# Transposing the second feed-forward's activation by VectorE in 32x32 blocks

## The chip, the cores and the metric

The kernel runs on one core of a Trainium2 chip, in one launch. The metric is the device time of one execution in microseconds (us): the median of three runs. PE is TensorE (matrix products, with PEld for its weight loads), DVE is VectorE, ACT is ScalarE, SP is the engine that issues the DMAs. Each engine works through its own instructions in the order in which the program emits them and waits for the others by semaphores.

## The reference, cut to what matters

The program is two transformer blocks of width 2048 over 256 tokens, float32. Each ends in a feed-forward of width 8192; the change touches the second one, whose result is the kernel's output:

```
h2 = rms_norm_2(x, norm2_w[l]) * (1.0 + scale2) + shift2
ff = jnp.square(jax.nn.relu(h2 @ w_ff1[l])) @ w_ff2[l]
x  = x + gate2 * ff
```

`scale2`, `shift2` and `gate2` come from a matrix product of a condition vector with `w_ada`, which the kernel does on VectorE.

## The kernel before, in words

**The stream.** All weights come from HBM as one stream of 1 MB blocks of 128 x 4 x 512 floats. A block has two halves, and a half-block holds two units; a unit is one 128x512 weight tile that is multiplied with the activations of both token tiles (`tt` 0 and 1, 128 tokens each). Float32 is split in two rounded parts: `prep_hi` (L183) lets ACT write the high part of a half-block (L201), `prep_lo` (L205) lets DVE write the remainder (L209). Each unit is then three products for each token tile (L303 to L305: high by high, high by low, low by high), so a half-block is 12 products. `hi` and `lo` have four buffers each (`HLB`), and `run` (L245) emits the split of a half-block three half-blocks before its products (`LOOK`).

**The second feed-forward** (`ffn`, L403) goes in four chunks `c` of 2048 hidden features. A chunk is first four segments of FF1 (512 hidden features each), then four segments of FF2 (512 output features each). A segment is 16 units, 8 half-blocks, in one accumulator per token tile. In chunk 0 the first two FF1 segments are interleaved block by block (`add_pair`), so that they end one half-block apart.

**The hand-over from FF1 to FF2.** When an FF1 segment's last product is emitted, `ff1_end` emits relu and square on ACT for both token tiles (L419, L420; tile `relu` in SBUF) and starts a generator `go`. FF2 needs this activation transposed, with the hidden features on the partitions. `split_to` (L343) does it for one token tile: four TensorE transposes into a PSUM tile `ms` (L348), ACT's copy to the high part (L349), DVE's subtraction for the low part (L350). The result is the tile `f`. FF2's segment for output group g reads `f` of the four FF1 segments in order, units 0 to 3 from the first, units 12 to 15 from the last.

**What sets the order.** Side work is written as generators. `step` (L238) advances each by one `yield`; `run` calls it twice in each half-block:

```
self.step()
...
self.prep_to(s + 1 + LOOK)
...
self.unit(*todo[0][0])
self.step()
self.unit(*todo[0][1])
```

`go` waits two yields (`lag(2)`), so its work stands in the program at the start of the second half-block after the segment's end. On ACT and DVE that lies between the splits of weights which belong to half-blocks three and four later.

**Other work on DVE here.** `ada_product` (L177) is a 128x2048 product and sum for the next modulation values, emitted ahead of the split of certain blocks: sixteen of these fall in chunks 0 and 1 (`ada2[80:]`, from block 302 on, one in two or three blocks; the second feed-forward is blocks 296 to 423). PSUM is used up: four buffers of `acc` and four of `ms`.

Of the kernel before, what the change touches and what calls it, by code (L numbers as in the profile page):

```python
# [8 lines left out]
F32 = mybir.dt.float32  # L9
# [5 lines left out]
ALU = mybir.AluOpType  # L15
# [3 lines left out]
P = 128  # L19
# [39 lines left out]
def lag(n):  # L59
    for _ in range(n):  # L60
        yield


class Net:
# [278 lines left out]
    def split_to(self, src, dst):  # L343
# [5 lines left out]
        nc.scalar.copy(dst[:, :, 0, :], ps)  # L349
        nc.vector.tensor_tensor(out=dst[:, :, 1, :], in0=ps, in1=dst[:, :, 0, :].bitcast(F32), op=ALU.subtract)  # L350

    def gate_rows(self, col, dst):

        nc = self.nc
        yield from lag(3)
        ps = self.ms([16, P])
        nc.tensor.transpose(ps, col, self.ident)
        row = self.t2([16, P], name="grow")
        nc.scalar.copy(row, ps)
        gd = self.dramp.tile([16, P], F32, tag="gd", name="gd")  # L360
        nc.sync.dma_start(out=gd, in_=row)
        yield from lag(3)
        nc.sync.dma_start(out=dst, in_=gd.rearrange("a b -> (a b)").partition_broadcast(P))
# [36 lines left out]
                norm.stats(0)  # L400


    def ffn(self, w1p, w1, w2, norm, mod, b, ada_base, next_norm=None, out=None):  # L403
        nc = self.nc
        first = len(self.subs)
        norm.attach(first)
        st = {}

        def pools():
            self.phase(fp=4, ffp=1)  # L410
        self.at(first, pools)

        def ff1_end(ft, g):
            def end(acc):
                f = ft[g] = self.fp.tile([P, 4, 2, S], F32R, tag="f", name="f")
                rs = []
                for tt in range(2):
                    r = self.t2(name="relu")
                    nc.scalar.activation(r, acc[tt], AF.Relu)  # L419
                    nc.scalar.activation(r, r, AF.Square)  # L420
                    rs.append(r)

                def go():
                    yield from lag(2)
                    for tt in range(2):
                        self.split_to(rs[tt], f[:, :, :, tt * P:(tt + 1) * P])
                self.spawn(go())
            return end

        def make_gate():  # L430
            assert self.ada_done >= ada_base + 96
            st["gate"] = self.ffp.tile([P, D], F32, tag="gate", name="gate2")
            col = self.mod_cols(mod, b, 80, "gate2c")
            yield
            yield from self.gate_rows(col, st["gate"])

        def early(g, c):
            def end(acc):
                if "sum" not in st:
                    st["sum"] = self.ffp.tile([P, 2, D], F32, tag="sum", name="fsum")  # L440
                cs = slice(g * 512, (g + 1) * 512)
                for tt in range(2):
                    d = st["sum"][:, tt, cs]
                    if c == 0:
                        nc.scalar.copy(d, acc[tt])
                    else:
                        nc.vector.tensor_tensor(out=d, in0=acc[tt], in1=d, op=ALU.add)
                if c == 2:
                    def go():
                        for tt in range(2):  # L450
                            yield from lag(2)
                            d, x = st["sum"][:, tt, cs], self.x[:, tt, cs]
                            nc.vector.tensor_tensor(out=d, in0=d, in1=st["gate"][:, cs], op=ALU.mult)
                            nc.vector.tensor_tensor(out=x, in0=x, in1=d, op=ALU.add)
                    self.spawn(go())
            return end

        def late(g):
            def end_tt(a, tt):
                self.residual(g, a, tt, st["gate"], next_norm)  # L460
                if out is not None:
                    cs = slice(g * 512, (g + 1) * 512)
                    nc.sync.dma_start(out=out[tt, :, cs], in_=self.x[:, tt, cs])
            return end_tt

        for c in range(4):
            ft = {}
            segs = [Seg(norm.lhs, range(16), ff1_end(ft, g)) for g in range(4)]
            if c == 0:
                self.add_pair([w1p[i] for i in range(8)], *segs[:2])  # L470
            else:
                for g in range(2):
                    self.add_seg([w1[4 * c + g, i] for i in range(4)], segs[g])
            for g in (2, 3):
                self.add_seg([w1[4 * c + g, i] for i in range(4)], segs[g])
            if c == 2:
                self.at(len(self.subs) - 24, lambda: self.spawn(make_gate()))
            f_lhs = self.lhs_of(lambda i, ft=ft: ft[i])
            for g in range(4):
                seg = Seg(f_lhs, range(16), early(g, c)) if c < 3 else Seg(f_lhs, range(16), end_tt=late(g), tail=4 if next_norm and g == 3 else 2)  # L480
                self.add_seg([w2[c, g, i] for i in range(4)], seg)
# [849 lines left out]
class Norm:  # L1331


    def __init__(self, net, w_name, mod, b, j_shift, j_scale, ada=0):
        self.n, self.w_name, self.mod, self.b, self.j, self.ada = net, w_name, mod, b, (j_shift, j_scale), ada
        self.ss = net.fix.tile([P, 2, 4], F32, tag="ss", name="ss", bufs=2)
        self.r = net.fix.tile([P, 2], F32, tag="nr", name="nr", bufs=2)
        self.get, self.lhs = net.act_tiles()
        self.xn = {}
        self.after = None  # L1340
# [77 lines left out]
def net(tc, A, out):  # L1418
    with ExitStack() as ctx:
        n = Net(ctx, tc, A)  # L1420
        with tc.manual_schedule():
            n.phase(mixp=1)
            n.setup()
            norm = n.block1()
            norm2 = Norm(n, "norm1_w_2", n.mod2, "b_ada_2", 0, 16, 96)
            n.ffn(A["ff1p_1"], A["ff1_1"], A["ff2_1"], norm, n.mod1, "b_ada", 0, next_norm=norm2)
            norm3 = Norm(n, "norm2_w_2", n.mod2, "b_ada_2", 48, 64, 96)
            n.block2(norm2, norm3)
            n.ffn(A["ff1p_2"], A["ff1_2"], A["ff2_2"], norm3, n.mod2, "b_ada_2", 96, out=out)
            ada2 = [(A["ada2"][j], j, n.mod2, lambda: n.cb) for j in range(96)]  # L1430
            r = n.ada_rest
            n.interleave([(37, 2, r[:4]), (45, 1.05, r[4:34]), (77, 3, r[34:36]), (83, 1, r[36:48]),
                          (100, 1.6, r[48:]), (127, 1, [n.load_c2]), (129, 1, [n.silu_c2]),
                          (130, 1.6, ada2[:58]), (230, 2.6, ada2[58:80]), (302, 2.5, ada2[80:])])
            n.run()
            n.scope.close()
# [118 lines left out]
```

## Time and profile before

| | |
|---|---|
| median of 3 runs | 2510.61 us (2510.32 to 2511.57) |
| profiled execution | 2512.52 us, span 2510.7 us |
| PE busy | 2478.9 us, 99% of the span |
| PE weight loads | 2047.1 us, 82% |
| DVE busy | 1807.3 us, 72% |
| ACT busy | 1259.9 us, 50% |

The span is what the hardware profiler saw of one execution. A busy time is the sum over an engine's instructions; products on PE overlap, so that one lasts 0.39 us while the next starts 0.23 us after it. Starts in a timeline are counted from the span's start. The FF1 segments of the second feed-forward end between about 1835 us (chunk 0) and 2418 us (the last of chunk 3).

### The profile page before, as it was taken

The numbers are of one execution on the slowest core, as the hardware profiler recorded it, in microseconds if no ns is written. First come the engines' busy times: TensorE is split into PE (matmuls) and PEld (weight loads), VectorE is DVE, ScalarE is ACT, GpSimd is POOL, SyncE is SP. The second block draws the span as 40 slices with busy tenths as digits, with TensorE's granted clock in tenths as the row PEclk, the third lists the DMA queues.
The fourth block names the chain that finished last, engine by engine and source line by source line (L and its number), as shares of the span: only waits on it lengthen the run. The fifth ranks groups of instructions, "written<-read, shape, count | busy, mean of one in ns | idle before, by whom it ended". The sixth has DMA issues, their size and how long they took to land.

```text
span 2510.7 us, 29213 instructions
## 1 busy us (share of the span) xinstructions
PE 2478.9 (99%) x11332; PEld 2047.1 (82%) x11332; DVE 1807.3 (72%) x2122; ACT 1259.9 (50%) x1727; POOL 4.0 (0%) x8
## 2 busy tenths in 40 slices
PE   7999999999999999999999999999999999999999
PEld 5778888887888888888887888888788888888887
DVE  7898888888875777787778878766676655456554
ACT  4536645445545444534446556665554453453443
POOL 0000000000000000000000000000000000000000
PEclk9999999999999999999999999999999999999999
DMA  9988678977887778787776655666567655555553
GB/s 358 369 322 318 243 297 323 394 306 286 303 317 284 303 315 316 287 333 306 294 276 222 249 214 211 221 232 223 212 252 278 259 200 194 208 185 191 193 190 130
DMA packets 93580, 666.24 MB, mean 265 GB/s; under 512 B 10817, under 2 KB 11521, under 8 KB 12929
## 3 DMA queue, kind: packets, MB, share of 16 engines
q1 hardware_dynamic: 93442, 664.38, 69.7%
q8 instruction: 89, 1.46, 0.2%
q14 instruction: 49, 0.40, 0.0%
HBM read 660.11 MB, written 4.23 MB: 265 GB/s over the span
## 4 chain that ended last, share of the span: by engine, by line
PE 88%; DVE 6%; ACT 3%; DMA 1%; issue 1%; SPq 0%; ACTq 0%; DVEq 0%
PE acc L303 28%; PE acc L305 28%; PE acc L304 28%; DVE lo L209 2%; DVE ada L177 2%; PE ms L348 1%; DMA raw<-in_win 1%; ACT hi L201 1%; PE ms L1178 1%; PE ms L855 1%; PE ms L1292 0%; ACT hm L1396 0%; PE ms L1410 0%; DVE res L395 0%; PE ms L762 0%
## 5 line engine op out<-in xcount | busy, mean ns | idle before, releaser
L209 DVE TENSOR_TENSOR lo<-raw,hi 128x1024 fp32r<-128x1024 f32 x848 | 1027.6, 1223 | 594.7 <-ACT hi L201 591.6
L201 ACT CAST hi<-raw 128x1024 fp32r<-128x1024 f32 x848 | 884.7, 1051 | 868.1 <-PE acc L305 825.0
L303 PE MATMUL acc<-hi,act 128*128 128x512 f32 x2208 | 875.5, 396 | 7.6 <-ACT hi L201 6.1
L304 PE MATMUL acc<-lo,act 128*128 128x512 f32 x2208 | 864.3, 391 | 9.8 <-DVE lo L209 9.8
L305 PE MATMUL acc<-hi,act 128*128 128x512 f32 x2208 | 863.1, 391 | 0.0
L304 PEld LDWEIGHTS acc<-lo,act 128*128 128x128 f32 x2208 | 416.3, 189 | 99.7 <-DVE lo L209 17.2
L303 PEld LDWEIGHTS acc<-hi,act 128*128 128x128 f32 x2208 | 416.2, 188 | 94.9 <-ACT hi L201 8.4
L305 PEld LDWEIGHTS acc<-hi,act 128*128 128x128 f32 x2208 | 415.9, 188 | 88.1 <-DVE act L1401 0.7
L177 DVE CUSTOM_DVE_ANT_0 ada<-ada,cb 128x2048 f32<-128x2048 f32 x192 | 438.3, 2284 | 0.5 <-DMA ada<-in_ada 0.5
L303 PE MATMUL acc<-hi,f 128*128 128x512 f32 x1024 | 399.1, 390 | 0.0
L305 PE MATMUL acc<-hi,f 128*128 128x512 f32 x1024 | 398.4, 389 | 0.0
L304 PE MATMUL acc<-lo,f 128*128 128x512 f32 x1024 | 398.4, 389 | 0.0
L305 PEld LDWEIGHTS acc<-hi,f 128*128 128x128 f32 x1024 | 192.2, 188 | 40.1
L304 PEld LDWEIGHTS acc<-lo,f 128*128 128x128 f32 x1024 | 192.2, 188 | 39.9
L303 PEld LDWEIGHTS acc<-hi,f 128*128 128x128 f32 x1024 | 192.2, 188 | 39.1
L384 ACT ACTIVATE act<-xT,sAB 128x256 fp32r<-128x256 f32 x16 | 9.6, 601 | 86.2 <-DVE sAB L565 86.2
L419 ACT ACTIVATE relu<-acc 128x512 f32<-128x512 f32 x64 | 37.7, 590 | 29.0 <-PE acc L305 29.0
L350 DVE TENSOR_TENSOR f<-ms,f 128x512 fp32r<-128x512 f32 x64 | 41.0, 683 | 3.1 <-ACT f L349 3.1
L395 DVE TENSOR_TENSOR res<-acc,gate 128x512 f32<-128x512 f32 x32 | 22.0, 689 | 28.2 <-PE acc L305 28.2
L398 ACT ACTIVATE res<-x 128x512 f32<-128x512 f32 x24 | 15.2, 633 | 52.6 <-DVE x L396 52.6
L420 ACT ACTIVATE relu<-relu 128x512 f32<-128x512 f32 x64 | 40.5, 633 | 2.0
L349 ACT CAST f<-ms 128x512 fp32r<-128x512 f32 x64 | 34.4, 589 | 13.8 <-PE ms L348 13.8
(245 smaller groups left out, 1266.8 us busy)
## 6 DMA issues: line engine op xcount, KB each, us to landing
raw<-in_ff SPq DMA_DIRECT2D x240, 1024.0 KB, 5.6
ada<-in_ada SPq DMA_DIRECT2D x192, 1024.0 KB, 5.8
raw<-in_win SPq DMA_DIRECT2D x120, 1024.0 KB, 6.5
raw<-in_ff1p SPq DMA_DIRECT2D x16, 1024.0 KB, 4.8
raw<-in_wa SPq DMA_DIRECT2D x8, 1024.0 KB, 6.9
raw<-in_wb SPq DMA_DIRECT2D x8, 1024.0 KB, 9.1
raw<-in_wop SPq DMA_DIRECT2D x8, 1024.0 KB, 6.9
raw<-in_wo SPq DMA_DIRECT2D x8, 1024.0 KB, 9.7
```

The costliest lines, as they stand in the source:

```text
L177: self.nc.vector.tensor_tensor_reduce(out=t, in0=t, in1=cb(), scale=1.0, scalar=0.0, op0=ALU.mult, op1=ALU.add, accum_out=mod[:, j:j + 1])
L201: self.nc.scalar.copy(hi, src)
L209: self.nc.vector.tensor_tensor(out=lo, in0=src, in1=hi.bitcast(F32), op=ALU.subtract)
L303: self.nc.tensor.matmul(a, xh, hi, start=first, stop=False)
L304: self.nc.tensor.matmul(a, xh, lo, start=False, stop=False)
L305: self.nc.tensor.matmul(a, xl, hi, start=False, stop=last)
L348: nc.tensor.transpose(ps[:, i, :], src[:, i * P:(i + 1) * P], self.ident)
L349: nc.scalar.copy(dst[:, :, 0, :], ps)
L350: nc.vector.tensor_tensor(out=dst[:, :, 1, :], in0=ps, in1=dst[:, :, 0, :].bitcast(F32), op=ALU.subtract)
L419: nc.scalar.activation(r, acc[tt], AF.Relu)
L420: nc.scalar.activation(r, r, AF.Square)
L855: mm = lambda *a, **kw: nc.tensor.matmul(*a, skip_group_check=True, **kw)
```

## The change

In the second feed-forward alone, `split_to` is replaced by a new generator `split_blocks`. For each token tile it issues 16 DVE transposes. Each takes 32 tokens (32 partitions) and, of each of the four groups of 128 features, the same 32 features (4 x 32 elements on each partition), transposes the four 32x32 blocks and writes them to 32 other partitions of a PSUM tile. Four transposes with the same tokens read the same 32 partitions and write one after the other to partitions 0, 32, 64 and 96; then the generator yields. After the fourth yield come the same ACT copy and DVE subtraction as before. The two token tiles are done one after the other, so that the generator now spans eight more yields, four half-blocks.

```diff
+    def split_blocks(self, src, dst):
+        nc = self.nc
+        t = self.ms([P, 4, P])
+        s4 = src.rearrange("p (g q f) -> p g q f", g=4, q=4)
+        for a in range(4):
+            ts = slice(32 * a, 32 * a + 32)
+            for q in range(4):
+                nc.vector.transpose(t[32 * q:32 * q + 32, :, ts], s4[ts, :, q, :])
+            yield
+        nc.scalar.copy(dst[:, :, 0, :], t)
+        nc.vector.tensor_tensor(out=dst[:, :, 1, :], in0=t, in1=dst[:, :, 0, :].bitcast(F32), op=ALU.subtract)
...
                 def go():
                     yield from lag(2)
                     for tt in range(2):
-                        self.split_to(rs[tt], f[:, :, :, tt * P:(tt + 1) * P])
+                        d = f[:, :, :, tt * P:(tt + 1) * P]
+                        if blocks:
+                            yield from self.split_blocks(rs[tt], d)
+                        else:
+                            self.split_to(rs[tt], d)
...
-            n.ffn(A["ff1p_2"], A["ff1_2"], A["ff2_2"], norm3, n.mod2, "b_ada_2", 96, out=out)
+            n.ffn(A["ff1p_2"], A["ff1_2"], A["ff2_2"], norm3, n.mod2, "b_ada_2", 96, out=out, blocks=True)
```

## Rows read from the trace of the kernel before

**Rows 1.** Page, part 1: busy time (share), instructions, of the whole span.

```profile
PE 2478.9 (99%) x11332; PEld 2047.1 (82%) x11332; DVE 1807.3 (72%) x2122; ACT 1259.9 (50%) x1727; POOL 4.0 (0%) x8
```

**Rows 2.** Waits, 1690 to 2510: who waited for whom, us, times, longest.

```profile
ACT hi L201 <- PE acc L305: 353.4, 220, 3.0
DVE lo L209 <- ACT hi L201: 311.1, 221, 3.1
...
PEld acc L304 <- DVE lo L209: 2.4, 4, 1.1
```

**Rows 3.** Source L348, 1690 to 2510: duration ns min/median/max, first and last start.

```profile
L348 PE MATMUL ms<-cst,relu x128: 270/272/273, 1838.5 to 2421.4; 128*128 128x128 f32 x128
```

**Rows 4.** Chain that ended last, 2380 to 2460: start, length, what.

```profile
2420.53 0.23 PE acc L305
2420.76 0.87 PE ms L348 x8
2421.64 0.23 PE acc L303
```

**Rows 5.** Timeline of ACT, 1830 to 1930: start, duration, instruction [idle before].

```profile
1829.83 1.98 ACT L201 CAST hi<-raw 128x1024 fp32r<-128x1024 f32 x2
...
1861.60 0.60 ACT L419 ACTIVATE relu<-acc 128x512 f32<-128x512 f32 x1 [0.98 <-PE acc L305]
...
1884.26 0.60 ACT L419 ACTIVATE relu<-acc 128x512 f32<-128x512 f32 x1 [0.98 <-PE acc L305]
...
1906.91 1.27 ACT L445 COPY fsum<-acc 128x512 f32<-128x512 f32 x2 [0.98 <-PE acc L305]
...
1928.67 1.27 ACT L445 COPY fsum<-acc 128x512 f32<-128x512 f32 x2 [0.98 <-PE acc L305]
```

**Rows 6.** Timeline of PE, from 2417.6: the last FF1 segment's end.

```profile
2417.65 0.39 PE L305 MATMUL acc<-hi,act 128*128 128x512 f32 x1
2417.88 0.39 PE L303 MATMUL acc<-hi,f 128*128 128x512 f32 x1
```

**Rows 7.** Timeline of ACT, 2417 to 2424, the same hand-over.

```profile
2417.40 0.60 ACT L419 ACTIVATE relu<-acc 128x512 f32<-128x512 f32 x1 [0.98 <-PE acc L305]
...
2419.72 1.03 ACT L201 CAST hi<-raw 128x1024 fp32r<-128x1024 f32 x1
2421.24 1.07 ACT L349 CAST f<-ms 128x512 fp32r<-128x512 f32 x2 [0.49 <-PE ms L348]
2422.20 1.06 ACT L201 CAST hi<-raw 128x1024 fp32r<-128x1024 f32 x1
```

**Rows 8.** Timeline of DVE, 2420 to 2425, the same hand-over.

```profile
2420.78 1.23 DVE L209 TENSOR_TENSOR lo<-raw,hi 128x1024 fp32r<-128x1024 f32 x1 [3.11 <-ACT hi L201]
2421.92 1.28 DVE L350 TENSOR_TENSOR f<-ms,f 128x512 fp32r<-128x512 f32 x2
```

**Rows 9.** Lines by form, DVE: busy us, mean ns, of 128-element and single-source instructions.

```profile
L350 DVE TENSOR_TENSOR f<-ms,f 128x512 fp32r<-128x512 f32 x64 | 41.0, 683 | 3.1 <-ACT f L349 3.1
...
L1014 DVE TENSOR_SCALAR lf<-ms,lb 128x128 f32<-128x128 f32 x16 | 5.3, 403 | 0.2 <-PE ms L1001 0.2
L754 DVE TENSOR_TENSOR ry<-qs,rope 128x128 f32<-128x128 f32 x8 | 2.3, 292 | 0.3
L1025 DVE TENSOR_SCALAR flow<-lf 128x512 f32<-128x512 f32 x4 | 1.7, 420 | 0.0
```

**Rows 10.** Timeline of DVE, 1376 to 1493: small instructions in a row.

```profile
1376.87 2.64 DVE L1014 TENSOR_SCALAR lf<-ms,lb 128x128 f32<-128x128 f32 x8 [0.18 <-PE ms L1001]
...
1489.80 0.29 DVE L754 TENSOR_TENSOR ry<-qs,rope 128x128 f32<-128x128 f32 x1
1490.01 0.22 DVE L755 TENSOR_TENSOR ry<-qs,rope 128x64 f32<-128x64 f32 x1
1490.14 0.22 DVE L756 TENSOR_TENSOR ry<-qs,rope 128x64 f32<-128x64 f32 x1
1490.40 0.29 DVE L757 TENSOR_TENSOR qs<-ry 128x128 f32<-128x128 f32 x1
```

**Rows 11.** Timeline of DVE, 1838 to 1893: first hand-over; an ada product.

```profile
1838.69 1.23 DVE L209 TENSOR_TENSOR lo<-raw,hi 128x1024 fp32r<-128x1024 f32 x1 [2.08 <-ACT hi L201]
...
1889.98 2.28 DVE L177 CUSTOM_DVE_ANT_0 ada<-ada,cb 128x2048 f32<-128x2048 f32 x1
1892.19 0.08 DVE L177 DVE_READ_ACCUMULATOR2_ANT mod<- 128x1 f32 x1
```

**Rows 12.** Busy times of stretches: PE, PEld, DVE, ACT, POOL; clock, DMA, GB/s.

```profile
1784.00:1838.00 54.00, 52.31 (x240) 41.53 (x240) 41.91 (x65) 37.12 (x61) 0.00 (x0) 1.00 0.58 216
...
2280.00:2345.00 65.00, 65.00 (x289) 53.81 (x288) 40.76 (x42) 25.05 (x25) 0.00 (x0) 1.00 0.54 192
```

More of the change, by code (lines that the diff above doesn't have):

```diff
@@ L400, in residual, with ffn @@
                 norm.stats(0)
-    def ffn(self, w1p, w1, w2, norm, mod, b, ada_base, next_norm=None, out=None):
+    def ffn(self, w1p, w1, w2, norm, mod, b, ada_base, next_norm=None, out=None, blocks=False):
         nc = self.nc
```

## The prediction

> **What bounds the kernel now.** I read the page's busy times first: PE is busy in 99% of the span, DVE in 72%, ACT in 50% [rows 1]. A busy PE is only half an answer, since products overlap, so the waits of the second feed-forward come next. There ACT waits for PE to give a `hi` buffer back, 353 us, and DVE waits for ACT's high part, 311 us, while PE's wait for DVE is 2.4 us [rows 2]: ACT and DVE follow PE, and each microsecond of PE work removed is a microsecond gained, as long as they keep up. The stretches say the same with the clock at its upper level, 2.4 GHz (granted 1.00): PE 65.0 us busy of 65, DVE 40.8. A stretch with gaps, PE 52.3 of 54 us, kept it too, so I add nothing for the clock [rows 12].
>
> Two paces follow. The ends of two FF2 segments lie 21.76 us apart, which is 2.72 us for a half-block; with a hand-over between them two FF1 segments lie 22.66 us apart [rows 5].
>
> **What the change removes.** 128 transposes on PE [rows 3], eight in each of 16 hand-overs. By the segments a hand-over costs PE 22.66 - 21.76 = 0.90 us [rows 5]; the chain has 0.87 us for its eight transposes [rows 4]. I take 16 x 0.90 = 14.4 us. That is the whole gain. ACT's copies and DVE's subtractions stay.
>
> **What it adds.** On DVE, 32 transposes for each segment, 512 in all. Call t the time from the start of one to the start of the next. The trace before has no DVE transpose, no DVE instruction on 32 partitions writing to 32 others of PSUM, so t is bounded by rows. Instructions of 128 elements per partition that don't depend on each other start 0.21 us apart with SBUF operands (1489.80 to 1490.01) and (2.64 - 0.40) / 7 = 0.32 us apart where one operand is in PSUM [rows 9, 10]. One that uses its predecessor's result starts when that has ended: 0.26 us after a start with 0.22 us length, 0.04 us more [rows 10]; with the 0.29 us of a 128-element instruction [rows 9] that is 0.33 us. The lower end: a single-source instruction does 512 elements in 0.42 us [rows 9], 0.27 us less than the 0.68 us that two-source ones take at one element per cycle, so two per cycle; 128 elements then save 0.07 us of the 0.21, t = 0.15 with a little rounding. The upper end: nothing overlaps and each lasts the 0.40 us of the PSUM one [rows 9]. I take t = 0.33: the two rows nearest in kind, PSUM operand and no overlap, give 0.32 and 0.33, and a transpose has to take in a block before it puts out its first row, so I expect no better overlap.
>
> The independent pair above overlapped (0.21 for a length of 0.29), but it kept to the same partitions. The Trainium skill ("VectorE: DVE Perf Modes", section "Two Vector instructions with no wait between them") speaks against this change: an instruction whose output starts in another group of 32 partitions than the last output in that memory is held until all earlier Vector instructions have finished. Each of the 512 transposes would be held; no run here shows it yet. By the pair t is 0.21 and the sum below -0.6 us, by the rule with the row's 0.29 us it is 0.33 and +54.4 us. The same page ("The three transpose paths") has 311 ns for a 128x128 DVE transpose; an estimate from that page with 0.04 us added is t = 0.35 and +64.6 us.
>
> **Where it lies.** DVE's time matters only if it makes PE wait. I follow one hand-over; S is the start of PE's first half-block after the segment (2417.88 [rows 6]). The split three half-blocks ahead starts on DVE at S + 2.90 (2420.78 [rows 8]), behind relu and square on ACT. Then, in program order: five weight remainders at 1.14 us (2421.92 - 2420.78 [rows 8]), 5.70 us; 16 transposes; a round trip to ACT for the copy of token tile 0, 0.80 us (0.59 us copy and, estimated, 0.2 us for two semaphores), with DVE standing still; its subtraction, 0.64 us (1.28 for two [rows 8]); 16 transposes; the second round trip and subtraction (0.80 + 0.68).
>
> *The last FF1 segment of a chunk.* FF2's unit 12 needs the low part of token tile 1 in its sixth product, at S + 6 x 2.72 + 5 x 0.227 = S + 17.45. It is ready at S + 2.90 + 8.62 + 32t: S + 22.1 for t = 0.33, 4.6 us late (before, the hand-over was done some 6 us after S [rows 8]). At t = 0.21 it is 0.8 us late.
>
> *Segment after segment.* ACT stands in the same queue: the copy of token tile 1 can't start before DVE's last transpose, and the next `hi` splits, the next relus and the `hi` after them are queued behind it. So there is a ring from one hand-over to the next: 5.70 + 16t + 1.44 + 16t on DVE, then on ACT 0.63 for the copy, three `hi` at 0.93 us (1.98 for two [rows 5]), four relu and square instructions 2.32 us (2419.72 - 2417.40 [rows 7]), one `hi` 1.08 us to its remainder. Sum 13.96 + 32t. PE's segment is 21.76 us, so the ring sets the pace above t = 0.244; at 0.33 it takes 24.52 us, 2.76 us per segment lost.
>
> *Chunks 2 and 3.* From the first hand-over to the last `f`: 2.90 + 3 (13.96 + 32t) + 8.62 + 32t = 53.40 + 128t, against 3 x 21.76 + 17.45 = 82.73 that PE needs without waits: 128t - 29.33 = 12.9 us each.
>
> *Chunk 1.* Three ada products, at blocks 334, 337 and 339; 334 and 339 stand among transposes, 337 beside ACT's part of the ring. Each holds DVE 2.21 us (1889.98 to 1892.19 [rows 11]): 128t - 24.91 = 17.3 us.
>
> *Chunk 0.* Two segments end together, so 64 transposes are queued at once. From the first hand-over (PE's first transpose, 1838.5 [rows 3]) DVE is free 1.3 us later (1838.69 + 1.14 [rows 11]); then 64t, five remainders 5.70, four subtractions 2.56, two round trips not covered by the other segment's work 1.60, one ada product 2.21, ACT's part 6.19; one ring 13.96 + 32t; the last leg 8.62 + 32t with another ada product 2.21. That is 44.35 + 128t against 2 x 21.76 + 17.45 = 60.97: 128t - 16.62 = 25.6 us.
>
> **The sum.** Waits 25.6 + 17.3 + 2 x 12.9 = 68.8 us, gain 14.4 us: +54.4 us. The profiled execution, 2512.5 us, becomes 2566.9; it stood 1.9 us above the median, so the median becomes 2565.0 us. A hundredth of a microsecond in t is worth 512 x 0.01 = 5.1 us. Costed at nothing: weight loads from HBM (a slower PE asks for less), the `relu` tiles and `ms` buffers held longer (two and one per token tile of four, the next segment's come eight half-blocks later), and PE's queue, which only loses work. What covers the DVE work up to t = 0.2 is the lead of three half-blocks; were it two, the cover would shrink by 2.72 us at each hand-over.
>
> **Rivals.**
> *Overlap (t = 0.20 to 0.26).* The transposes follow each other like independent SBUF instructions; they do write different bytes. For it: 0.21 us in rows 10. Against it: the 0.32 us spacing with PSUM in the same rows. At 0.21: chunk 0 loses 10.3, chunk 1 2.0, the last segments of chunks 2 and 3 0.8 each, 13.8 against 14.4: 2510.0 us, no change. At 0.25: 27.9 of waits, 2524.1 us.
> *Hidden, and faster.* The transposes run at two elements per cycle, t = 0.15. Only chunk 0's double hand-over then loses, 2.6 us: 2498.8 us. It decides from t below 0.195. For it: DVE's idle third [rows 12] and the single-source row. Against: PSUM output, and the transposing itself.
> *No overlap and a dearer instruction (t = 0.40).* 34.6 + 26.3 + 2 x 21.9 = 104.7 us of waits, 2600.9 us; for it the 0.40 us of the PSUM row, which has scalar operands that a transpose lacks.
>
> **How the numbers follow.** The forecast, t = 0.29 to 0.37 (2544 to 2585 us), 56%; overlap 19%, some half of it above t = 0.227; faster 8%; t of 0.38 and more 17%. Within 0.2% of 2510.6, 5.0 us, about what a measurement of this kernel can tell from no change, means t between 0.195 and 0.227. So faster 0.09, same 0.11, slower 0.80. The range runs from 2511 to 2604 us: it leaves out the faster case, the lower edge of the overlap and the upper part of the dear one, some 2 in 10.
>
> **What would show it.** In the trace after: 512 transposes on DVE with starts 0.33 us apart (0.21 would be the overlap, 0.15 the faster one); PE waiting in FF1 of chunks 1 to 3 for `lo` and `hi` near each segment's end, and 4 to 7 us for `f` in the seventh half-block of each chunk's FF2, the most in chunk 0; FF1 segments 24 to 25 us apart in place of 22.66; FF2 segments after the first unchanged at 21.76. The prediction is wrong if PE doesn't wait for `f`, or if t is right and the segments still keep 21.76 us: then ACT and DVE don't form the ring.

## The result, and the profile after

The changed kernel takes 2586.85 us (median of 4 runs, 2584.42 to 2588.45) against 2511.09 us before: ratio 1.0299, 95% interval 1.0286 to 1.0312, 75.8 us slower. The forecast was 2565.0 us in a range from 2511 to 2604: the sign and the mechanism came out, the size was 54.4 us where 75.8 were measured.

The page of the profile after, busy times as in [rows 1]; then the lines of its costliest groups that answer to [rows 2, 3] (busy us, mean ns of one, idle time before them and what ended it).

```profile
span 2586.6 us, 29438 instructions
...
PE 2494.2 (96%) x11204; PEld 2041.1 (79%) x11204; DVE 1969.8 (76%) x2634; ACT 1252.4 (48%) x1727; POOL 4.0 (0%) x8
...
PE 73%; DVE 18%; ACT 6%; issue 3%; DMA 1%; ACTq 0%; SPq 0%; DVEq 0%
...
L304 PE MATMUL acc<-lo,act 128*128 128x512 f32 x2208 | 870.6, 394 | 40.0 <-DVE lo L209 40.0
...
L303 PE MATMUL acc<-hi,f 128*128 128x512 f32 x1024 | 404.3, 395 | 17.6 <-ACT f L362 16.8
...
L360 DVE STREAM_TRANSPOSE ms<-relu 32x128 f32<-32x128 f32 x512 | 165.3, 323 | 16.9
```

128 products on PE have gone (11332 to 11204), 512 instructions on DVE have come (2122 to 2634), each 0.323 us long. DVE is busy in only 76% of the span, yet it holds 18% of the chain that ended last, where it had 6%: PE now stands idle 40 us before FF1's products that need `lo` (9.8 us before the change), and 16.8 us before products that need `f`.

The waits of the second feed-forward, as in [rows 2]: who waited for whom, us, times, longest.

```profile
ACT hi L201 <- PE acc L305: 226.8, 145, 3.0
ACT f L362 <- DVE ms L360: 217.8, 32, 9.1
DVE lo L209 <- ACT hi L201: 181.5, 150, 2.7
PEld acc L304 <- DVE lo L209: 58.0, 41, 4.9
PE acc L304 <- DVE lo L209: 41.7, 38, 4.2
...
PE acc L303 <- ACT f L362: 16.8, 4, 5.4
```

ACT follows PE for a shorter time than before (227 for 353 us). Its new wait is for DVE's transposes, 32 times, some 7 us each, and while it stands there the next weight splits stand behind it.

One hand-over after another in chunk 3, on DVE (start, duration, instruction [idle before]), to be read beside [rows 8].

```profile
2451.18 1.39 DVE L360 STREAM_TRANSPOSE ms<-relu 32x128 f32<-32x128 f32 x4
2452.48 1.20 DVE L209 TENSOR_TENSOR lo<-raw,hi 128x1024 fp32r<-128x1024 f32 x1
2453.71 2.82 DVE L360 STREAM_TRANSPOSE ms<-relu 32x128 f32<-32x128 f32 x8
2456.56 1.23 DVE L209 TENSOR_TENSOR lo<-raw,hi 128x1024 fp32r<-128x1024 f32 x1
2457.81 1.41 DVE L360 STREAM_TRANSPOSE ms<-relu 32x128 f32<-32x128 f32 x4
2459.87 0.69 DVE L363 TENSOR_TENSOR f<-ms,f 128x512 fp32r<-128x512 f32 x1 [0.65 <-ACT f L362]
2460.82 3.50 DVE L209 TENSOR_TENSOR lo<-raw,hi 128x1024 fp32r<-128x1024 f32 x3 [0.25 <-ACT hi L201]
2465.97 1.23 DVE L209 TENSOR_TENSOR lo<-raw,hi 128x1024 fp32r<-128x1024 f32 x1 [1.65 <-ACT hi L201]
2467.22 1.39 DVE L360 STREAM_TRANSPOSE ms<-relu 32x128 f32<-32x128 f32 x4
...
2491.41 1.23 DVE L209 TENSOR_TENSOR lo<-raw,hi 128x1024 fp32r<-128x1024 f32 x1 [1.65 <-ACT hi L201]
```

Eight transposes take 2.82 us, so (2.82 - 0.32) / 7 = 0.357 us from start to start: that is t. The remainder at 2465.97 and its successor one segment later, 2491.41, are 25.44 us apart. ACT in the same stretch, to be read beside [rows 7]:

```profile
2459.25 0.59 ACT L362 CAST f<-ms 128x512 fp32r<-128x512 f32 x1 [6.92 <-DVE ms L360]
2459.74 2.94 ACT L201 CAST hi<-raw 128x1024 fp32r<-128x1024 f32 x3
2462.58 0.60 ACT L432 ACTIVATE relu<-acc 128x512 f32<-128x512 f32 x1
...
2488.02 0.60 ACT L432 ACTIVATE relu<-acc 128x512 f32<-128x512 f32 x1
```

Copy, three `hi`, relu without a gap: ACT's part of the ring. The relus of two segments are 25.44 us apart, where they were 22.66.

What the forecast didn't have is seen on PE. The first FF2 segment of chunk 1, in its seventh half-block:

```profile
2119.65 0.40 PE L305 MATMUL acc<-hi,f 128*128 128x512 f32 x1
2125.46 0.79 PE L303 MATMUL acc<-hi,f 128*128 128x512 f32 x1 [5.42 <-ACT f L362]
```

and in chunk 3, the products after such a wait, with the stretches around them (length; busy us of PE, PEld, DVE, ACT, POOL; granted clock, DMA share, GB/s):

```profile
2512.64 0.63 PE L304 MATMUL acc<-lo,f 128*128 128x512 f32 x1
2513.06 0.63 PE L305 MATMUL acc<-hi,f 128*128 128x512 f32 x1
...
2518.92 0.39 PE L305 MATMUL acc<-hi,f 128*128 128x512 f32 x1
2519.14 0.39 PE L303 MATMUL acc<-hi,f 128*128 128x512 f32 x1
```

```profile
2511.00:2516.00 5.00, 5.00 (x12) 3.85 (x13) 4.09 (x5) 2.65 (x3) 0.00 (x0) 0.50 0.46 175
2517.00:2519.00 2.00, 2.00 (x10) 1.60 (x10) 1.99 (x3) 0.39 (x1) 0.00 (x0) 1.00 0.95 353
```

After the wait the granted clock is 0.50, the lower level of 1.2 GHz, and products start 0.43 us apart; then it is back at 1.00 and they start 0.23 us apart. In the whole stretch 77 products run at the lower level, in seven groups of 7 to 13, each group behind waits of PE: two behind waits for `lo` of 3.7 and 4.2 us in chunk 0, one behind 3.2 us for `lo` in chunk 1, three behind the 5.4 us for `f` of chunks 0, 1 and 2, the last behind 2.4 us for `lo` and 0.5 us for `f` in chunk 3. Before the change there was none. The longest of the waits for `lo`:

```profile
1865.39 0.80 PE L304 MATMUL acc<-lo,act 128*128 128x512 f32 x1 [4.21 <-DVE lo L209]
```

### The profile page after: what moved, and what is told of

The parts are those of the page before. It is cut to its first block, busy times and chain, and to the rows that moved or that the text cites. A ratio compares the mean times of both kernels' runs of the same rounds, so it can differ in the third digit from the quotient of the medians.

```text
span 2586.6 us, 29438 instructions
## 1 busy us (share of the span) xinstructions
PE 2494.2 (96%) x11204; PEld 2041.1 (79%) x11204; DVE 1969.8 (76%) x2634; ACT 1252.4 (48%) x1727; POOL 4.0 (0%) x8
## 4 chain that ended last, share of the span: by engine, by line
PE 73%; DVE 18%; ACT 6%; issue 3%; DMA 1%; ACTq 0%; SPq 0%; DVEq 0%
PE acc L303 23%; PE acc L304 23%; PE acc L305 23%; DVE lo L209 6%; DVE ms L360 6%; DVE ada L177 3%; ACT hi L201 3%; PE ms L1195 1%; PE ms L872 1%; PE ms L348 1%; DVE f L363 0%; ACT f L362 0%; ACT relu L432 0%; PE ms L1309 0%; DMA raw<-in_win 0%
## 5 line engine op out<-in xcount | busy, mean ns | idle before, releaser
L303 PE MATMUL acc<-hi,f 128*128 128x512 f32 x1024 | 404.3, 395 | 17.6 <-ACT f L362 16.8
L305 PE MATMUL acc<-hi,f 128*128 128x512 f32 x1024 | 402.2, 393 | 0.0
L360 DVE STREAM_TRANSPOSE ms<-relu 32x128 f32<-32x128 f32 x512 | 165.3, 323 | 16.9
L362 ACT CAST f<-ms 128x512 fp32r<-128x512 f32 x32 | 18.8, 586 | 217.8 <-DVE ms L360 217.8
L432 ACT ACTIVATE relu<-acc 128x512 f32<-128x512 f32 x64 | 37.7, 590 | 18.2 <-PE acc L305 18.2
```

The source lines that it names most:

```text
L303: self.nc.tensor.matmul(a, xh, hi, start=first, stop=False)
L305: self.nc.tensor.matmul(a, xl, hi, start=False, stop=last)
L360: nc.vector.transpose(t[32 * q:32 * q + 32, :, ts], s4[ts, :, q, :])
```

## The experiments

Theory: DVE's transposes don't overlap, DVE and ACT form a ring longer than PE's segment, and FF2 waits for the last `f`. Rivals were other reasons for t, other reasons for the waits, and the clock. Ratios are to the kernel before, run on the same chip.

**Why 0.357 us: the partitions written.**

```diff
-                nc.vector.transpose(t[32 * q:32 * q + 32, :, ts], s4[ts, :, q, :])
+                nc.vector.transpose(t[ts, :, 32 * q:32 * q + 32], s4[ts, :, q, :])
```

> The DVE transposes keep their number, size and order, but each writes to the 32 partitions that it reads (the columns are exchanged in its place), so the move to other partition groups is left out and f is not the transposed activation. Four transposes in a row then read and write the same 32 partitions. Theory (what sets the 0.35 us from start to start is that the partitions written change from one to the next, so that each starts when the one before has ended): duration still 0.32 us, but starts 0.22 to 0.25 us apart within a group of four; with t = 0.24 the prediction's sum is +9 us and the time about 2515 to 2528 us. Rival (a transpose doesn't let its successor start early, wherever it writes): starts 0.35 us apart as in the changed kernel, time 2580 to 2592 us.

Measured: 2585.28 us, ratio 1.030 (1.0282 to 1.0317), the changed kernel's time. Four transposes with the same 32 partitions for reading and writing still take 1.36 us:

```profile
2465.38 1.36 DVE L360 STREAM_TRANSPOSE ms<-relu 32x128 f32<-32x128 f32 x4
2466.66 1.19 DVE L209 TENSOR_TENSOR lo<-raw,hi 128x1024 fp32r<-128x1024 f32 x1
2467.88 2.81 DVE L360 STREAM_TRANSPOSE ms<-relu 32x128 f32<-32x128 f32 x8
```

That is 0.35 to 0.36 us from start to start: my theory fell, in this kernel something else is enough to keep them apart.

**The loops exchanged** (`for q` outside, `for a` inside).

> The two loops are exchanged: four transposes in a row write to the same 32 partitions and read from 32 others each. The result is the same. Theory (a change of the partitions read or of the partitions written is enough to hold the next transpose): starts 0.35 us apart, time within 6 us of 2587. Rival (only the partitions written count): 0.24 us apart within a group of four, 0.27 on the mean, time about 2530 to 2545 us. If the same-partition run keeps 0.35 us as well, both fall.

Measured: 2588.13 us (one run), eight transposes in 2.83 us, 0.36 us apart. After the run above it says nothing by itself on the partitions.

**A plain copy in the transpose's place.**

```diff
-                nc.vector.transpose(t[32 * q:32 * q + 32, :, ts], s4[ts, :, q, :])
+                nc.vector.tensor_copy(t[ts, :, 32 * q:32 * q + 32], s4[ts, :, q, :])
```

> As the same-partitions run, but each transpose is a plain DVE copy of the same 32 x 128 elements from the same SBUF partitions to the same place in PSUM, so nothing is transposed in FF2's activation. The same-partitions run kept 0.35 us from start to start. Theory (it is the transposing that keeps the next from starting early): copies start 0.20 to 0.24 us apart, and with t = 0.22 the waits nearly vanish: 2505 to 2520 us. Rival (32 partitions, or PSUM as the place written, hold the next instruction): copies 0.30 us or more apart, 2545 us or more.

Measured: 2571.24 us (one run); copies of the same shape last 0.290 us and start (2.56 - 0.29) / 7 = 0.32 us apart:

```profile
L360 DVE COPY ms<-relu 32x128 f32<-32x128 f32 x512 | 148.7, 290 | 17.0
...
2455.61 2.56 DVE L360 COPY ms<-relu 32x128 f32<-32x128 f32 x8
```

So it isn't the transposing, and the rival holds. The list of the program's instructions with their waits then showed why: within a burst each instruction that writes to the PSUM tile waits for a semaphore of DVE itself, that is for the one before it, although they write different bytes; the independent pair of [rows 10] has no such wait. The traces agree: in this run and in the changed kernel the second, third and fourth instruction of each group of four carry that wait.

```
L360 COPY ms<-relu 32x4x32
L360 COPY ms<-relu 32x4x32 [waits DVE_49] x3
...
L773 TENSOR_TENSOR ry<-qs,rope 128x4x16
```

0.32 - 0.29 = 0.03 us is close to the gap that [rows 10] has for an instruction with such a wait, 0.04.

**Without that wait, to SBUF.** This needs the wide kernel told of below: one transpose for both token tiles, 32 x 256 elements, to SBUF; the program puts no wait between the transposes of a group there. In the experiment the place written is again the partitions read.

```diff
-                nc.vector.transpose(t[32 * q:32 * q + 32, :, ts], s8[ts, :, q, :])
+                nc.vector.transpose(t[ts, :, 32 * q:32 * q + 32], s8[ts, :, q, :])
```

> As the wide run with slack, but each transpose writes to the 32 partitions that it reads (the move between groups is left out). The program has no semaphore wait between the four transposes of a group here, since they write to SBUF; in the PSUM kernels each carries a wait for the one before. Theory A (without such a wait, a change of the partitions read or written still holds the next instruction): in the wide run starts are 0.45 us apart at a length of 0.44; here they come to 0.33 to 0.38 us within a group of four. Theory B (a transpose never lets the next one start early, wait or not): 0.44 to 0.45 us here too. The time says nothing on it, since DVE is not the bound: within 3 us of the wide run with slack.

The lines of the wide kernel, then of this one (busy us, mean ns), and a burst of each.

```profile
L372 DVE STREAM_TRANSPOSE cb<-cb 32x256 f32<-32x256 f32 x128 | 55.8, 436 | 1.9
...
2361.06 3.58 DVE L372 STREAM_TRANSPOSE cb<-cb 32x256 f32<-32x256 f32 x8
```

```profile
L372 DVE STREAM_TRANSPOSE cb<-cb 32x256 f32<-32x256 f32 x128 | 45.3, 404 | 0.6
...
2349.74 2.84 DVE L372 STREAM_TRANSPOSE cb<-cb 32x256 f32<-32x256 f32 x8
```

With a change of partitions (3.58 - 0.44) / 7 = 0.449 us apart at a length of 0.436: no overlap, though nothing waits. Without it (2.84 - 0.40) / 7 = 0.349 apart at a length of 0.404: overlap. The same run shows both: inside a group of four, where the partitions stay, starts are 0.33 to 0.37 us apart; from the last transpose of a group to the first of the next, where they change, 0.405 us. Theory A holds. So two things keep the transposes of the change apart, and either is enough: the program's wait on the PSUM tile, and the change of partitions. Transposes to PSUM in the same partitions and without that wait were not run. The time, 2502.2 us (one run) against 2517.6 of the wide kernel, was not within 3 us: there DVE's place in the ring did count, as the last experiment explains.

**The wait for f, taken away.**

```diff
-                        if blocks:
+                        if blocks and g < 3:
```

> The last of the four FF1 segments of each chunk is transposed by PE as before, the other three by DVE. Theory (two separate costs: the ring of DVE and ACT between hand-overs, and the wait for f in the seventh half-block of FF2): the four waits for f (5.4 us each in the changed kernel) and the slow products behind them go, 0.9 us of PE per chunk comes back, the segments of FF1 stay 25.4 us apart between DVE hand-overs; about 30 us less, 2550 to 2565 us. Rival (the wait for f only stands where DVE's backlog would be waited for anyway): the time stays within 8 us of 2587, and the wait for lo grows by what the wait for f loses.

Measured: 2560.21 us, ratio 1.0195 (1.0180 to 1.0210), 26.6 us less than the change.

```profile
PE acc L304 <- DVE lo L209: 37.7, 33, 4.8
```

No wait for `f` is left, the wait of PE's products for `lo` is 37.7 us for 41.7, FF1's relus after a DVE hand-over still come 25.44 us apart (2390.61, 2416.05, 2441.49), and 33 products run at the lower clock for 77. Two separate costs, as the theory had it.

**The clock after the wait.**

```diff
+                if blocks and g == 3:
+                    def busy():
+                        yield from lag(12)
+                        ps = self.ms()
+                        a = ft[0][:, 0, :, :].rearrange("p a b -> p (a b)")
+                        for i in range(16):
+                            nc.tensor.matmul(ps, ft[0][:, 0, 0, 0:P], a, start=True, stop=True)
+                    self.spawn(busy())
```

> The changed kernel with 16 extra products of 128x512 on PE (their result is not used) just ahead of unit 12 of each chunk's first FF2 segment, where PE waits 5.4 us for f: 3.6 us of work at the upper clock, inside the wait. Theory (after the wait the granted clock is 0.50 for about 5 us, 8 to 13 products at 0.43 us in place of 0.23, and that is what the prediction's sum lacks beside t): with PE at work during most of the wait the clock stays at the upper level, the time falls by 4 to 9 us, to 2578 to 2583 us. Rival (the clock is of no account, or falls because of the earlier waits for lo): same time within 3 us of 2587, slow products as before.

Measured: 2581.13 us, ratio 1.0277 (1.0262 to 1.0293), 5.7 us less with 64 products more. The intervals of the two ratios touch, but the trace is plain: some 30 products at the lower clock for 77. Behind the waits for `f` six are left, in chunk 1, where 2.53 us of the wait remain; in chunks 0, 2 and 3 there are none. The others stand in chunk 0, behind waits for `lo`. The count varies with much the same waits: the run with the partitions kept has 57 in place of 77, so not all of the difference is the extra products' work.

```profile
2123.39 0.80 PE L303 MATMUL acc<-hi,f 128*128 128x512 f32 x1 [2.53 <-ACT f L362]
...
2499.02 3.79 PE L451 MATMUL ms<-f 128*128 128x512 f32 x16
...
2506.02 0.50 PE L303 MATMUL acc<-hi,f 128*128 128x512 f32 x1 [0.49 <-ACT f L362]
2506.36 0.39 PE L304 MATMUL acc<-lo,f 128*128 128x512 f32 x1
```

**Half of the work on DVE.** Token tile 0 by DVE, token tile 1 by PE (`if blocks and c and tt == 0`).

> Token tile 0 is transposed by DVE, token tile 1 by PE, in chunks 1 to 3; chunk 0 wholly by PE. Theory (DVE's work costs nothing while the ring of DVE and ACT stays shorter than PE's segment): the ring is 13.96 + 16 x 0.357 = 19.7 us, under 21.76, f of token tile 0 is ready some 13 us after the segment, before it is needed at 16.3; 12 x 0.45 = 5.4 us of PE saved, 2505 to 2508 us. Rival (any DVE transposes among the weight splits delay PE): 2511 us or more.

Measured: 2515.18 us, ratio 1.0015 (1.0006 to 1.0024). The function runs when `c` already has its last value, so chunk 0 was split half and half too, and its two hand-overs at once kept PE waiting. With the chunk's number handed in as an argument:

> Token tile 0 by DVE (32 x 128, to PSUM, as the change has it), token tile 1 by PE, in chunks 1 to 3; chunk 0 by PE. (In the earlier half run the exception for chunk 0 had no effect: the condition saw the last chunk's number, and all four chunks were split half and half; its waits for lo were all in chunk 0.) Theory: ring 19.7 us, nothing waits, 12 x 0.45 = 5.4 us saved: 2505 to 2508 us. Rival (the half run's loss was not chunk 0's double hand-over): 2513 us or more.

Measured: 2508.82 us, ratio 0.9988 (0.9979 to 0.9997), just above the 2505 to 2508 us expected. In chunk 3 the relus come 22.26 and 22.22 us apart, 21.76 + 0.45 as expected; in chunk 1, beside the ada products, 23.14 and 22.89, so that most of the saving of that chunk is lost.

**Both token tiles in one instruction.** Relu writes both token tiles side by side into one SBUF buffer, so that half as many transposes do twice as much, and one copy and one subtraction follow.

```diff
+        s8 = src.rearrange("p (h q f) -> p h q f", h=8, q=4)
+        for a in range(4):
+            ts = slice(32 * a, 32 * a + 32)
+            for q in range(4):
+                nc.vector.transpose(t[32 * q:32 * q + 32, :, ts], s8[ts, :, q, :])
+            yield
```

> In chunks 2 and 3 the two token tiles lie side by side in SBUF, and each transpose takes both: 16 transposes of 32 partitions x 256 elements for a segment in place of 32 of 128, written to SBUF in place of PSUM, one copy and one subtraction of 1024 elements behind them; chunks 0 and 1 wholly by PE. Theory: a transpose costs 0.19 us plus one element per cycle plus 0.03 us to the next start, so 256 elements 0.49 us, 7.8 us per segment for 11.4; the ring is 20.9 us, under 21.76, and f is ready at 16.6 us against 16.8 to 17.5 needed; 8 x 0.9 = 7.2 us saved, at most 2 us of waits for f: 2503 to 2506 us. Rival (transposes take more than a cycle per element, so that joining them saves nothing: 0.71 us each): ring 24.5 us, the waits of the changed kernel for two chunks, 2520 to 2530 us.

> The wide transposes in chunks 2 and 3 and, in chunk 1, token tile 0 by DVE in 32 x 128 pieces; chunk 0 by PE. Theory: both savings add, 7.2 + 4 x 0.45 = 9.0 us, less some 2 us where ada products stand among chunk 1's transposes: 2502 to 2505 us. Rival: chunk 1's ada products use up the lead, nothing or a loss beside the wide run.

By the same slip both ran as one kernel: all 16 segments wide, and in chunks 0 and 1 the buffer is the ada products' operand, so that part of the modulation is computed from other data. 2533.28 us (1.0090, 1.0076 to 1.0104) and 2533.69 us. What they give is the length: 0.436 us for 256 elements where 128 took 0.323, so that joining saves. With the chunk's number handed in, buffers that are free in each chunk, and 13 of the 16 segments:

> The wide transposes (32 x 256, both token tiles in one, SBUF to SBUF) where DVE has room: third segment of chunk 0 and all segments of chunks 1 to 3, 13 of 16; the rest by PE. The buffers are free in those chunks, so the result is the reference's. Theory: at 0.45 us from start to start (the wide run) the transposes of a segment are 7.2 us, the ring 5.70 + 7.2 + 1.15 + 6.19 = 20.2 us, under PE's 21.76, f ready 16.0 us after the segment, before 16.8; 13 x 0.90 = 11.7 us saved, up to 2 us lost to ada products in chunks 0 and 1: 2499 to 2502 us. Rival (DVE's transposes cost PE time wherever they stand among the weight splits): 2508 us or more.

Measured: 2517.57 us, ratio 1.0024 (1.0016 to 1.0033): slower than before, where a gain was expected. The rival seemed right, but the trace names the place. ACT in chunk 3:

```profile
2359.59 1.06 ACT L201 CAST hi<-raw 128x1024 fp32r<-128x1024 f32 x1 [1.66 <-PE acc L305]
2367.75 1.05 ACT L376 CAST f<-cb 128x1024 fp32r<-128x1024 f32 x1 [7.11 <-DVE cb L372]
2368.70 3.89 ACT L201 CAST hi<-raw 128x1024 fp32r<-128x1024 f32 x4
```

The copy stands in ACT's queue ahead of the seventh half-block's split and waits 7.1 us for DVE; PE then waits 0.59 us for that half-block's low part.

```profile
2371.25 0.50 PE L304 MATMUL acc<-lo,act 128*128 128x512 f32 x1 [0.59 <-DVE lo L209]
```

In chunks 2 and 3 that only eats the gain: the relus come 22.65 us apart, as before the change. The loss stands in chunk 1, beside the ada products, where the first three come 24.88 and 26.51 us apart and PE waits up to 2.81 us:

```profile
2036.94 0.50 PE L304 MATMUL acc<-lo,act 128*128 128x512 f32 x1 [2.81 <-DVE lo L209]
```

My sum had compared the ring with the segment and had not looked at the lead inside it.

**The copy one yield later.**

```diff
+        yield
         v = t.rearrange("p (t g) n -> p g t n", t=2)
```

> The wide run with slack and one more yield between the last transpose and ACT's copy, so that one more weight split (hi and lo of the seventh half-block) stands ahead of the copy on ACT. In the wide run ACT's copy waits 7 us for DVE's last transpose, that split stands behind it, and PE waits for its low part, 0.6 to 0.9 us in each segment, which is what the change saves. Theory (the place in ACT's queue is what costs): these waits go, f is ready 16.4 us after the segment, just before 16.8: 13 x 0.90 = 11.7 us saved, up to 2 us lost to ada products: 2499 to 2503 us, below the kernel before. Rival (DVE's work itself is too long, and the wait only moves to f or to the next split): 2511 us or more.

Measured: 2500.64 us, ratio 0.9959 (0.9945 to 0.9973): 10.8 us less than before, the best of all. ACT in chunk 3, and what is left of PE's waits:

```profile
2349.63 1.05 ACT L201 CAST hi<-raw 128x1024 fp32r<-128x1024 f32 x1 [1.66 <-PE acc L305]
2355.08 1.05 ACT L377 CAST f<-cb 128x1024 fp32r<-128x1024 f32 x1 [4.39 <-DVE cb L372]
2356.04 2.94 ACT L201 CAST hi<-raw 128x1024 fp32r<-128x1024 f32 x3
...
2362.55 0.60 ACT L452 ACTIVATE cb<-acc 128x512 f32<-128x512 f32 x1 [0.98 <-PE acc L305]
```

```profile
PE acc L304 <- DVE lo L209: 1.8, 4, 0.7
```

The split now stands ahead of the copy, ACT waits 2.7 us less, and the relus (2340.79, 2362.55) come 21.76 us apart, PE's own pace with no transposes in it.

## Why the prediction was right, and where it was short

*The gain, 14.4 us.* Right: without waits a hand-over costs PE nothing (21.76 us in the last run), and 13 of 16 gave 10.8 of 11.7 us.

*t = 0.33.* A little low, for a reason that was half wrong, and most of what the forecast lacked: it measured 0.357 because the instruction lasts 0.323 us and not 0.29, plus 0.03. The transposes don't overlap, as I took it, but not because a transpose takes in a block first: in the same partitions and without a wait they do overlap (0.349 for 0.404). The program's wait on the PSUM tile, which I had not looked for, and the change of partitions each do it. The second is the rule of the Trainium skill, "VectorE: DVE Perf Modes", section "Two Vector instructions with no wait between them"; the pair 0.449 and 0.349 agrees with it. By the same section of the Trainium skill an instruction is held, too, when an input of it starts in another group of 32 partitions than the first input of the last instruction that read that memory. `lo` in the timeline after agrees with that: behind the first four transposes (tokens 0 to 31, partitions from 0, as `lo` reads) it starts 0.09 us before their end (2451.18 + 1.39 against 2452.48), behind the next eight, which read other partitions, 0.03 us after it. The 311 ns that the prediction takes from the Trainium skill (the same page, section "The three transpose paths") are stated for bf16 with SBUF as the place written; float32 to PSUM took 323 ns here. 0.027 us more in t is 13.8 us by the prediction's sum: 54.4 + 13.8 = 68.2, which leaves 7.6 of the 75.8 us.

*The ring, 13.96 + 32t.* Right: 25.38 at the measured t, 25.44 measured. Its parts are less exact than the sum, and here the errors cancel: a `lo` ahead of transposes takes 1.23 to 1.26 us to the next start where 1.14 was put, and a round trip to ACT 0.65 us where 0.80 was put, whose 0.2 us for semaphores no run shows; and the `lo` behind the first four transposes starts before the last of them has ended. The three rivals fall with t. In the wide kernel, with the ring shorter than the segment, the same working missed the copy's place in ACT's queue; where a ring is safe, the lead at each point of it still has to be followed.

*The waits by chunk.* Counted between the first relus of the chunks, with 0.9 us added for each transposed segment: 31.7, 24.0, 18.0 and 17.3 us (186.69 - 158.64 + 3.6, 198.01 - 177.65 + 3.6, 192.20 - 177.84 + 3.6, 174.91 - 161.26 + 3.6). The prediction's terms at t = 0.357 are 29.1, 20.8, 16.4 and 16.4. The terms stand in the right order; 8.3 us are missing in these two profiled executions.

*"I add nothing for the clock".* This is the step that failed. The stretch that I read for it [rows 12] had only short gaps; behind waits of 2.4 to 5.4 us the clock came back at its lower level, 77 products took 0.20 us more each, 15 us in all, of which a part stood beside waits anyway. Keeping PE at work through the wait for `f` alone gave 5.7 us back by the medians. In that run's trace the four figures are 29.3, 22.7, 16.5 and 14.7 us, 83.2 together, where the terms give 82.7. So most of the missing time went as the slow products went. By chunk, 1.9 us too many in chunk 1 and 1.7 too few in chunk 3 stay open, and since the count of slow products varies, the sum fits in part by luck. What the slow products behind waits for `lo` cost was not tried.

*What would show it.* PE's waits for `f` and `lo`, the longer segments and FF2 at 21.76 us came as told. In size, starts were 0.357 us apart for 0.33, and segments 25.44 us for 24 to 25, in chunk 1 up to 28.13 beside the ada products. The waits for `f` were not the most in chunk 0: 5.4 us in each of three chunks; in chunk 3 2.4 us for `lo` came first and 0.5 for `f`.

## What to carry to other kernels

An engine that is idle a third of the time is not free: what counts is the lead that it has where the work is put, and what is queued behind each instruction that waits for it, on the other engines too. Before work is moved to small instructions, look up their spacing, not only their length, and whether the program makes each wait for the one before; wider instructions pay: one for both token tiles took 0.449 us from start to start, two narrow ones 2 x 0.357. Moving one copy behind one more weight split turned a kernel 6 us slower than before into one 11 us faster.

## What the runs showed of the hardware that was not expected

- A DVE transpose of 32 partitions costs 0.323 us for 128 float32 elements to PSUM and 0.436 us for 256 to SBUF, 0.404 us where it stays in its partitions. An estimate from these, though the places written differ: more than half of the 0.323 us doesn't depend on the number of elements.
- A plain copy of 32 x 128 elements to PSUM lasts 0.290 us, only a tenth less than the transpose.
- Behind a wait of 5.42 us PE's first 12 products in chunk 1 ran at the lower clock; with 3.8 us of extra products in the wait, six did.
- With no wait between them, a transpose that writes to other partitions than the one before starts after that one's end (0.449 us apart, 0.436 long), one that stays starts before it (0.33 to 0.37 apart, 0.404 long).
